# Feature-major weight chunks taken in pairs: the order of high and low products on TensorE

## The chip, the cores and the metric

One core of a Trainium2 chip runs the whole program in one launch. The metric is the device time in microseconds (us) of that launch; a lower number is better. Engines are named as in the profile: PE is TensorE (PEld its weight loads), ACT is ScalarE, DVE is VectorE, POOL is GpSimd, SP is the engine that issues the weight transfers.

## The reference, cut to what matters

Two transformer-like blocks are applied to one sequence of 256 tokens and 2048 features, all in float32. The first block normalises the input, projects it (`h @ w_in[l]`, 12040 columns), runs three sequence mixers (S5, HGRN2 and mLSTM), merges them through gates and `w_out`, and ends with a convolutional feed-forward network. The second block does the same with a dense and a dilated attention. Nearly all of the arithmetic is large matrix products with these weights:

```python
        h = rms_norm(x, mix_norm[l])
        (u_a, q_b, f_b, i_b, og_b, cx_c, v_c, o_c, ig_c, fg_c, gates) = jnp.split(h @ w_in[l], splits, axis=-1)
        ...
        x = x + merged @ w_out[l]
        x = x + conv_ffn(rms_norm(x, ffn_norm[l]), ffn_w_up[l], ffn_conv_w[l], ffn_conv_b[l], ffn_w_down[l])
```

## The kernel before, in words

**Linears, groups, chunks.** Every weight matrix is a linear with a name of its own (`w_qf`, `w_up`, `w_dn`, ...). `_linears` (L67) cuts its output columns into groups. A group of kind T ("feature-major") has two blocks of 128 output features; the weights are the stationary operand and the activations the moving one. A group of kind K ("token-major") has up to 512 output columns; there the weights move. `_chunks` (L124) cuts the input features of a group into chunks: a chunk of a T group with two blocks holds 4 input tiles of 128, so 8 pairs of (input tile, output block). A linear with 2048 input features has 4 chunks a group, one with 5632 has 11.

**High and low parts.** The float32 weights are split for accuracy. `prep` (L357) does it for one chunk: SP loads `wraw`, ACT writes the rounded part `whi` (L365), DVE writes the rest `wlo = wraw - whi` (L366). The activations are split as well: a moving operand is [high 256 | low 256] of the tokens. `mm` (L371) then issues, for a T chunk, 8 high products (`whi` against 512 moving columns, L389) and 8 low products (`wlo` against the 256 high columns, L386). The two kinds are kept in runs: `self.part` remembers which kind was issued last, and a chunk that doesn't open its accumulators begins with that kind. So chunk 0 of a group goes high, low; chunk 1 low, high; chunk 2 high, low; chunk 3 low, high; the next group begins high again. Runs are 16 long, and 8 long at the joint of two 11-chunk groups, where chunk 10 ends low and the next group has to open with high.

**The order of the program.** `run` (L457) walks over all 1009 chunks in one list, `self.seq`. For chunk i it does, in this order: `step()`, `prep` of chunk i+3, `mm` of chunk i, and behind the last chunk of a group its `evac`. All queues are in program order. `step` (L444) advances everything else by one stage: the mixers' generators ("lanes") and the deferred epilogues ("loose"). A stage can hold PE instructions, which then stand in PE's queue between the products of chunk i-1 and those of chunk i. The pools for `wraw`, `whi`, `wlo` have 4 buffers each, the accumulators 2.

**The stages that the steps of the prediction touch**, with the chunks' numbers in `self.seq`:

- `w_qf` (chunks 9 to 32), `w_cx` and `w_og` (65 to 84), beside the S5 mixer. `s5` (L912) works on 16 slices. For each it issues L1126 on PE (input products), DVE operations L1130 to L1145, and two stages after L1145 the output products L1151 on PE. In this stretch the PE stages fall on chunks 24, 28, 32, 68, 72, 76, 80, 84, between chunks 2 and 3 of a group (counted from 0).
- `w_oo` (149 to 164), beside the mLSTM mixer, whose four heads issue L1474 and L1475 on PE at chunks 150, 152, 154, 156. They need a PSUM bank that DVE's L1477 of the head before frees, and the first needs `kz`, written by ACT at L488. Two chunks later follow L1481 to L1483.
- `w_out` and `w_o`, each at the end of a branch: `turn_split` (L517) transposes the last 512 merged features on PE (L526) in the stage of chunk 1 of the first group, after DVE's L839 or L1797 has finished them and L532 has freed the PSUM bank.
- `v_c`: `norms` (L1639) sums squares over features on PE (L563) in the stage of chunk 3 of the first group, after POOL's L1613.
- `w_up` (44 groups, `ev_up` L1566): the evacuation goes ACT L405, DVE L406, DVE L416, ACT L1574, DVE L1580, ACT L1622, POOL L1624.
- `w_down` and `w_dn`: 8 groups of 11 chunks each. `w_gu` has 44 groups of 4, `w_out` and `w_o` 8, `w_qf` 6, `v_c` and `w_oo` 4, `w_cx` 3, `w_og` 2.

Of the kernel before, what the change touches and what calls it, by code (L numbers as in the profile page):

```python
# [123 lines left out]
def _chunks(lin):  # L124

    out = []
    for kind, tiles in lin["groups"]:
        widths = [len(t) for t in tiles]
        ks = np.arange(len(lin["k"]))
        n = -(-len(ks) // (1024 // sum(widths)))  # L130
        cs = [list(c) for c in np.array_split(ks, n)]
        if lin.get("early"):
            cs[:1] = [[k] for k in cs[0]]
        out.append((kind, widths, cs))
    return out
# [166 lines left out]
class Chunk:  # L302
    def __init__(self, src, off, pitch, w, mms, group):
        self.src, self.off, self.pitch, self.w, self.mms, self.group = src, off, pitch, w, mms, group
        self.first = self.last = False
        self.pre = self.post = self.hl = None


class Group:
# [4 lines left out]
class Kernel:  # L314
# [7 lines left out]
    def add(self, name, operand, evac, before=None):  # L322
        lin = LIN[name]
        nk, off = len(lin["k"]), 0
        for g, (kind, widths, chunks) in enumerate(_chunks(lin)):
            tot = sum(widths)
            grp = Group(kind, operand, (lambda *b, g=g: evac(g, *b)), (lambda g=g: before(g)) if before else None)
            for ci, ks in enumerate(chunks):
                mms = []
                for n, k in enumerate(ks):  # L330
                    c = n * tot
                    for j, w in enumerate(widths):
                        mms.append((k, j, c, w, k == 0, k == nk - 1))
                        c += w
                if ci == len(chunks) - 1:
                    mms.sort(key=lambda m: m[1] // 2)
                ch = Chunk(self.a[name], off, len(ks) * tot, len(ks) * tot, mms, grp)
                ch.first, ch.last = ci == 0, ci == len(chunks) - 1
                self.seq.append(ch)
                off += len(ks) * tot * P  # L340

# [29 lines left out]
    def mm(self, ch):  # L371


        nc, g = self.nc, ch.group
        while 2 * len(g.acc) <= max(m[1] for m in ch.mms):
            g.acc.append(self.pm.tile([P, 2, 2, S], F32, name="acc"))
        hi, lo = ch.hl
        if g.kind == "T":
            for b in range(len(g.acc)):
                mine = [m for m in ch.mms if m[1] // 2 == b]  # L380

                order = (1, 0) if self.part and not any(m[4] for m in mine) else (0, 1)
                for n, e in enumerate(order):
                    for k, j, c, w, st, en in mine:
                        if e:
                            nc.tensor.matmul(g.acc[b][:, j % 2, 0], lo[:, c:c + w], g.operand(k)[:, 0], start=False,  # L386
                                             stop=en and n == 1, skip_group_check=True)
                        else:
                            nc.tensor.matmul(g.acc[b][:, j % 2], hi[:, c:c + w], g.operand(k), start=st,  # L389
                                             stop=en and n == 1, skip_group_check=True)  # L390
                self.part = order[1]
            return
        self.part = 0
        for k, j, c, w, st, en in ch.mms:
            x = g.operand(k)
            for th in range(2):
                out = g.acc[0][:, th].rearrange("p a b -> p (a b)")[:, :w]
                t = slice(th * P, th * P + P)
                for n, (e, y) in enumerate(((0, hi), (1, hi), (0, lo))):
                    nc.tensor.matmul(out, x[:, e, t], y[:, c:c + w], start=st and n == 0, stop=en and n == 2,  # L400
                                     skip_group_check=True)
# [55 lines left out]
    def run(self):  # L457
        nxt, due = 0, 0
        for i, ch in enumerate(self.seq):
            if ch.first and ch.group.before:  # L460
                ch.group.before()
            due += ch.w
            if due >= 1024:
                self.step()
                due -= 1024
            while nxt < len(self.seq) and nxt <= i + self.LOOKAHEAD:
                self.prep(self.seq[nxt])
                nxt += 1
            self.mm(ch)
            if ch.last:  # L470
                ch.group.evac(*ch.group.acc)
        while self.loose or any(self.lanes.values()):
            self.step()
# [1154 lines left out]
    def build_second(self):  # L1628
# [163 lines left out]
        def ev_o(br, n, acc):  # L1792
            s = self.half_of(t[f"s{br}"], n)
            v.tensor_tensor(s, self.flat2(acc), s, op=OP.mult)
            if br:
                m = self.half_of(t["s0"], n)
                (v if n == 3 else gp).tensor_tensor(m, m, s, op=OP.add)  # L1797
                mm = t.setdefault("mm", [])
                mm.append(big("mm", (4, 2, S), F32R))
                self.defer(self.turn_split(mm, 4 * n, m, 1 if n == 3 else 2))  # L1800
# [292 lines left out]
```

## Time and profile before

| what | value |
|---|---|
| time, median of 3 runs | 2929.17 us (2928.81 to 2929.7) |
| the profiled execution's own time | 2929.41 us |
| its span, first to last instruction | 2927.6 us |
| PE busy | 2892.3 us, 99% of the span |
| PEld busy | 2522.4 us, 86% |
| DVE busy | 1944.2 us, 66% |
| ACT busy | 1454.2 us, 50% |
| POOL busy | 387.9 us, 13% |
| mean granted TensorE clock | 0.996 |

A busy PE is not a PE at its peak, since matmuls overlap and their ends are modelled. What counts for this kernel is the spacing of the starts of its matmuls. A line of the timeline gives the start of a run of equal instructions, the time to the end of its last one, the engine, the line of the kernel, what it writes and reads, the shape and the count; in brackets stands how long the engine was idle before it and what ended the wait. The time that a run takes of PE is the difference between its start and the start of the next run.

### The profile page before, as it was taken

Reading aid. Unit: us, or ns where it says so; the run is one execution under the profiler, and the core shown is the slowest. Engines: PE = TensorE matmul, PEld = TensorE weight load, DVE = VectorE, ACT = ScalarE, POOL = GpSimd, SP = SyncE. Lnnn points to the kernel's source line nnn. Section 1 sums busy time; section 2 is a strip of 40 time slices with the busy share of each in tenths; the row PEclk is TensorE's granted clock in tenths of the full one; section 3 lists DMA queues with packets and bytes.
Section 4 is the critical chain, followed back from the end, with each engine's and each line's share of the span. In section 5 each row is a group of like instructions: output and inputs, shape, how many; then the busy total and the mean of one; then the engine's idle time right before and its main releaser. Section 6 shows DMA issues by size and latency. Waiting matters only on the chain.

```text
span 2927.6 us, 41008 instructions
## 1 busy us (share of the span) xinstructions
PE 2892.3 (99%) x15682; PEld 2522.4 (86%) x15682; DVE 1944.2 (66%) x2536; ACT 1454.2 (50%) x2066; POOL 387.9 (13%) x412
## 2 busy tenths in 40 slices
PE   7999999999999999999999999999999999999999
PEld 6898888888888888888888988888888888888888
DVE  8998785655777777775556665565776655555444
ACT  5654545444455555554444654554544444444332
POOL 6120240011111111110111040100220000000000
PEclk9999999999999999999999999999999999999999
DMA  6565554565655555556655665565665555555664
GB/s 213 177 185 172 162 169 137 180 190 189 208 176 194 188 188 191 190 194 199 198 190 182 200 188 161 170 195 179 194 202 186 190 184 196 183 198 187 202 197 141
DMA packets 155606, 543.39 MB, mean 186 GB/s; under 512 B 17904, under 2 KB 20336, under 8 KB 155408
## 3 DMA queue, kind: packets, MB, share of 16 engines
q1 hardware_dynamic: 148752, 524.16, 55.9%
q10 hardware_dynamic: 4224, 8.21, 0.9%
q0 software_dynamic: 2432, 8.39, 0.9%
q8 instruction: 123, 2.02, 0.3%
q14 instruction: 75, 0.61, 0.1%
HBM read 534.92 MB, written 4.19 MB: 184 GB/s over the span
## 4 chain that ended last, share of the span: by engine, by line
PE 95%; DVE 3%; POOL 1%; ACT 1%; issue 1%; DMA 0%; ACTq 0%; DVEq 0%; POOLq 0%
PE acc L389 41%; PE acc L400 29%; PE acc L386 21%; PE ps_s L1298 1%; DVE wlo L366 1%; PE ps_s L1151 1%; PE ps_s L2021 0%; POOL s5p L931 0%; POOL s5p L926 0%; PE ps_s L1868 0%; PE ps_s L526 0%; ACT whi L365 0%; PE ps_s L2014 0%; PE ps_s L1949 0%; PE ps_s L1968 0%
## 5 line engine op out<-in xcount | busy, mean ns | idle before, releaser
L366 DVE TENSOR_TENSOR wlo<-wraw,whi 128x1024 fp32r<-128x1024 f32 (+3 forms) x1009 | 1261.9, 1264 | 765.8 <-ACT whi L365 760.9
L365 ACT ACTIVATE whi<-wraw 128x1024 fp32r<-128x1024 f32 (+3 forms) x1009 | 1035.0, 1040 | 854.2 <-PE acc L400 361.3
L389 PE MATMUL acc<-z,whi 128*128 128x512 f32 x2816 | 672.8, 391 | 0.0
L389 PEld LDWEIGHTS acc<-z,whi 128*128 128x128 f32 x2816 | 517.6, 188 | 100.1
L386 PEld LDWEIGHTS acc<-z,wlo 128*128 128x128 f32 x2816 | 361.0, 191 | 13.7
L386 PE MATMUL acc<-z,wlo 128*128 128x256 f32 x2816 | 365.3, 283 | 0.0
L389 PE MATMUL acc<-act,whi 128*128 128x512 f32 x1408 | 337.3, 391 | 0.0
L400 PE MATMUL acc<-whi,x 128*128 128x512 f32 (+2 forms) x1024 | 305.6, 379 | 0.0
L389 PEld LDWEIGHTS acc<-act,whi 128*128 128x128 f32 x1408 | 258.4, 188 | 49.7
L400 PE MATMUL acc<-whi,y 128*128 128x512 f32 (+2 forms) x960 | 289.3, 383 | 0.0
L1624 POOL TENSOR_TENSOR conv<-conv 128x256 f32<-128x256 f32 x88 | 100.7, 1145 | 882.1 <-ACT conv L1622 455.7
L400 PEld LDWEIGHTS acc<-whi,x 128*128 128x128 f32 x1024 | 188.8, 188 | 29.2 <-ACT whi L365 0.5
L400 PEld LDWEIGHTS acc<-whi,y 128*128 128x128 f32 x960 | 176.1, 188 | 28.3
L400 PE MATMUL acc<-wlo,x 128*128 128x512 f32 (+2 forms) x512 | 193.4, 378 | 2.1 <-DVE wlo L366 2.1
L386 PEld LDWEIGHTS acc<-act,wlo 128*128 128x128 f32 x1408 | 181.6, 191 | 7.5
L386 PE MATMUL acc<-act,wlo 128*128 128x256 f32 x1408 | 183.9, 283 | 0.0
L400 PE MATMUL acc<-wlo,y 128*128 128x512 f32 (+2 forms) x480 | 181.2, 377 | 0.0
L389 PE MATMUL acc<-x,whi 128*128 128x512 f32 x544 | 138.7, 404 | 9.7 <-ACT whi L365 6.5
L389 PEld LDWEIGHTS acc<-x,whi 128*128 128x128 f32 x544 | 103.1, 196 | 29.4 <-ACT whi L365 6.5
L400 PEld LDWEIGHTS acc<-wlo,x 128*128 128x128 f32 x512 | 96.4, 188 | 18.0 <-DVE wlo L366 2.4
L400 PEld LDWEIGHTS acc<-wlo,y 128*128 128x128 f32 x480 | 90.1, 188 | 15.6
L1622 ACT ACTIVATE conv<-conv 128x256 f32<-128x256 f32 x88 | 36.7, 418 | 131.5 <-DVE conv L1580 69.1
(455 smaller groups left out, 2901.2 us busy)
## 6 DMA issues: line engine op xcount, KB each, us to landing
wraw<-w_up SPq DMA_DIRECT2D x176, 512.0 KB, 3.7
wraw<-w_gu SPq DMA_DIRECT2D x176, 512.0 KB, 4.2
wraw<-w_down SPq DMA_DIRECT2D x88, 512.0 KB, 3.9
wraw<-w_dn SPq DMA_DIRECT2D x88, 512.0 KB, 4.0
wraw<-w_g SPq DMA_DIRECT2D x64, 512.0 KB, 3.9
wraw<-v_g SPq DMA_DIRECT2D x64, 512.0 KB, 3.5
wraw<-w_b SPq DMA_DIRECT2D x32, 512.0 KB, 4.3
wraw<-w_out SPq DMA_DIRECT2D x32, 512.0 KB, 4.0
```

The source lines that it names most:

```text
L365: nc.scalar.activation(hi[:, :w], raw[:, :w], AF.Copy)
L366: nc.vector.tensor_tensor(lo[:, :w], raw[:, :w], hi[:, :w].bitcast(F32), op=OP.subtract)
L386: nc.tensor.matmul(g.acc[b][:, j % 2, 0], lo[:, c:c + w], g.operand(k)[:, 0], start=False, stop=en and n == 1, skip_group_check=True)
L389: nc.tensor.matmul(g.acc[b][:, j % 2], hi[:, c:c + w], g.operand(k), start=st, stop=en and n == 1, skip_group_check=True)
L400: nc.tensor.matmul(out, x[:, e, t], y[:, c:c + w], start=st and n == 0, stop=en and n == 2, skip_group_check=True)
L1151: nc.tensor.matmul(py[T][:, 0], zc[:, e, 96 - 32 * j:224 - 32 * j], X[:, 3 + e], start=j + e == 0, stop=j + e == 4, skip_group_check=True)
L1298: nc.tensor.matmul(ps[:, i, b], ks[:, h, c], q[:, h, c if m < 8 else slice(P, S)], start=i + b == 0, stop=True, skip_group_check=True)
L1622: nc.scalar.activation(s, s, AF.Silu)
L1624: nc.gpsimd.tensor_tensor(s, s, c[:, 1], op=OP.mult)
```

## The change: what it does

The second chunk of each pair in a two-block T group of more than one chunk gets the first as its `mate`, and the first is `held`: its `mm` issues nothing. The `mm` of the second issues the products of both: the high ones of both chunks and then the low ones of both, or the other way round where the kind issued last was low. The eleventh chunk of an 11-chunk group stays alone. In `run` the products of a chunk with a mate are issued before the `prep` of chunk i+3 instead of behind it, because that `prep` takes the buffers of the held chunk.

```diff
 class Chunk:
-        self.pre = self.post = self.hl = None
+        self.pre = self.post = self.hl = self.mate = None
+        self.held = False
 ...
 (add)
                 ch.first, ch.last = ci == 0, ci == len(chunks) - 1
+                if kind == "T" and len(widths) == 2 and ci % 2 and not (chunks[0] is chunks[-1]):
+                    ch.mate = self.seq[-1]
+                    ch.mate.held = True
                 self.seq.append(ch)
 ...
 (mm)
-        hi, lo = ch.hl
         if g.kind == "T":
-            for b in range(len(g.acc)):
-                mine = [m for m in ch.mms if m[1] // 2 == b]
-
-                order = (1, 0) if self.part and not any(m[4] for m in mine) else (0, 1)
+            if ch.held:
+                return
+            both = [ch.mate, ch] if ch.mate else [ch]
+            tiles = [(2 * b, 2 * b + 1) for b in range(len(g.acc))]
+            for js in tiles:
+                b = js[0] // 2
+                mine = [(*x.hl, *m) for x in both for m in x.mms if m[1] in js]
+
+                order = (1, 0) if self.part and not any(m[6] for m in mine) else (0, 1)
                 for n, e in enumerate(order):
-                    for k, j, c, w, st, en in mine:
+                    for hi, lo, k, j, c, w, st, en in mine:
 ...
         self.part = 0
+        hi, lo = ch.hl
 ...
 (run)
                 self.step()
                 due -= 1024
+            if ch.mate:
+
+                self.mm(ch)
             while nxt < len(self.seq) and nxt <= i + self.LOOKAHEAD:
                 self.prep(self.seq[nxt])
                 nxt += 1
-            self.mm(ch)
+            if not ch.mate:
+                self.mm(ch)
```

## Rows read from the trace of the kernel before

**Rows 1.** The page: busy time of the engines; chain that ended last, by engine
```profile
PE 2892.3 (99%) x15682; PEld 2522.4 (86%) x15682; DVE 1944.2 (66%) x2536; ACT 1454.2 (50%) x2066; POOL 387.9 (13%) x412
...
PE 95%; DVE 3%; POOL 1%; ACT 1%; issue 1%; DMA 0%; ACTq 0%; DVEq 0%; POOLq 0%
```

**Rows 2.** Timeline of PE in `w_up` (start, us, engine, line, ...)
```profile
1199.99 3.82 PE L389 MATMUL acc<-z,whi 128*128 128x512 f32 x16
1203.65 2.08 PE L386 MATMUL acc<-z,wlo 128*128 128x256 f32 x16
1205.56 3.82 PE L389 MATMUL acc<-z,whi 128*128 128x512 f32 x16
```

**Rows 3.** Timeline of PE at the joint of two groups of `w_down`
```profile
1342.82 1.11 PE L386 MATMUL acc<-act,wlo 128*128 128x256 f32 x8
1343.77 2.00 PE L389 MATMUL acc<-act,whi 128*128 128x512 f32 x8
1345.61 1.60 PE L386 MATMUL acc<-act,wlo 128*128 128x256 f32 x12
```

**Rows 4.** Timeline of PE at the start of `w_out`
```profile
731.14 2.02 PE L389 MATMUL acc<-mo,whi 128*128 128x512 f32 x8
...
734.70 1.29 PE L526 MATMUL ps_s<-ident,m 128*128 128x128 f32 x8 [0.59 <-DVE mo L532]
```

**Rows 5.** Timeline of PE at the start of `w_o`
```profile
2095.16 1.98 PE L389 MATMUL acc<-mm,whi 128*128 128x512 f32 x8
...
2098.97 1.06 PE L526 MATMUL ps_s<-ident,m 128*128 128x128 f32 x8 [0.89 <-DVE m L1797]
```

**Rows 6.** Timeline of PE at the start of `v_c`
```profile
1558.15 2.00 PE L389 MATMUL acc<-y,whi 128*128 128x512 f32 x8
...
1566.52 1.84 PE L563 MATMUL ps_s<-ones,acc 128*128 128x1 f32 x16
```

**Rows 7.** Timeline of POOL in the same stretch
```profile
1563.93 1.94 POOL L1613 TENSOR_TENSOR acc<-acc,sq 128x512 f32<-128x512 f32 x1 [0.31 <-ACT sq L1605]
```

**Rows 8.** Timeline of PE in `w_cx` and `w_og`: S5's output products
```profile
205.40 1.02 PE L1151 MATMUL ps_s<-s5s,s5z 128*128 128x256 f32 x4
...
233.47 2.04 PE L1151 MATMUL ps_s<-s5s,s5z 128*128 128x256 f32 x4 [3.45 <-DVE s5s L1145]
...
247.38 1.02 PE L1151 MATMUL ps_s<-s5s,s5z 128*128 128x256 f32 x4
```

**Rows 9.** Timeline of DVE there: the operation that L1151 needs
```profile
203.75 0.78 DVE L1145 TENSOR_TENSOR s5s<-s5s 128x512 f32<-128x512 f32 x1
...
244.87 0.69 DVE L1145 TENSOR_TENSOR s5s<-s5s 128x512 f32<-128x512 f32 x1
```

**Rows 10.** Timeline of PE in `w_oo`
```profile
468.72 1.98 PE L389 MATMUL acc<-x,whi 128*128 128x512 f32 x8
...
472.34 0.70 PE L1475 MATMUL ps_s<-qk,kz 128*128 128x256 f32 x2 [0.27 <-ACT kz L488]
...
481.35 0.70 PE L1474 MATMUL ps_s<-qk 128*128 128x256 f32 x2 [2.31 <-DVE E L1477]
...
490.88 0.59 PE L1474 MATMUL ps_s<-qk 128*128 128x256 f32 x2
```

**Rows 11.** Timeline of DVE in `w_oo`
```profile
489.88 0.55 DVE L1477 SCALAR_TENSOR_TENSOR E<-ps_s,E 128x384 f32<-128x384 f32 x1
```

**Rows 12.** Timeline of PE in `w_qf`
```profile
65.33 1.39 PE L386 MATMUL acc<-x,wlo 128*128 128x256 f32 x8 [4.24 <-DVE wlo L366]
```

**Rows 13.** Windows: stretch, us, busy of PE, PEld, DVE, ACT, POOL, granted clock, DMA
```profile
482.60:486.00 3.40, 3.40 (x15) 3.11 (x15) 1.56 (x2) 0.00 (x0) 0.00 (x0) 0.51 0.60 169
```

**Rows 14.** Timelines of ACT and DVE in `w_up`
```profile
923.70 0.60 ACT L405 ACTIVATE pad<-acc 128x512 f32<-128x512 f32 x1 [1.99 <-PE acc L389]
...
927.86 1.23 DVE L366 TENSOR_TENSOR wlo<-wraw,whi 128x1024 fp32r<-128x1024 f32 x1 [2.11 <-ACT whi L365]
```

**Rows 15.** Groups by line and shape (count, busy us, mean ns, idle us before, releaser)
```profile
L386 PE MATMUL acc<-x,wlo 128*128 128x256 f32 x544 | 77.9, 292 | 7.5 <-DVE wlo L366 7.5
```

## The prediction

> **What bounds the kernel now.** I read the page first, for the engine that the end hangs on. PE is busy 99% of the span, and 95% of the chain that ended last lies on it [rows 1]. So the time is what PE's queue takes, instruction by instruction, and the next view is PE's timeline: the spacing in long stretches without a wait, then every place where something other than weight products stands in the queue.
>
> In `w_up`, 16 high products take 1203.65 - 1199.99 = 3.66 us of PE and 16 low ones 1205.56 - 1203.65 = 1.91 us [rows 2]: 5.57 us for two chunks, 2.78 us for one. Nothing waits there. The reader is to see that PE's other work, the mixers' small products, sits between chunks, and that it is ready with little to spare or already late when PE comes to it [rows 4 to 6, 8, 10].
>
> **The change, part by part.**
>
> *Longer runs.* The trace has no run of 32, so I extrapolate from 8 to 16. At a joint of `w_down` 8 low products take 0.95 us and 8 high ones 1.84 us [rows 3]. Twice that is 5.58 us against 5.57 us for runs of 16 [rows 2]: by kind, 3.68 against 3.66 and 1.90 against 1.91. The rounding is as large as the difference, so one pair of runs less is worth 0.01 to 0.03 us; I take 0.02. A group of 4 chunks goes from two pairs of runs to one: 6 + 3 + 2 + 4 + 8 + 44 + 4 + 8 + 44 = 123 groups, from `w_qf` to `w_gu`. A group of 11 chunks goes from six to three, and there are 16: 48 more. 171 x 0.02 = 3.4 us saved (1.7 to 5.1).
>
> By the rows the spacing in a run is 3.66 / 16 = 229 ns and 1.91 / 16 = 119 ns [rows 2], and hardly depends on the run's length. The Trainium skill (TensorE: Matmul & The Clock Gate, Back-to-back issue gap) gives 518 and 262 cycles at the full clock for 512 and 256 columns, which is 216 and 109 ns. By that the sum for two chunks would be 5.2 us, and if what is above it came from the changes of kind, halving these would return about 0.37 us for each of 171, some 63 us. The rows speak against it, since 8 or 16 in a run cost the same for each product; it is the last rival below.
>
> *What the pairing moves.* The number of products, transfers, ACT and DVE operations is unchanged, and ACT, DVE, POOL and SP keep their order; SP's transfers wait on DVE alone as before. PE's queue does change. `step()` still runs once for each chunk, but a held chunk issues nothing behind it. So PE work of a step at a held chunk stays where it was, while PE work of a step at the second of a pair now stands ahead of both chunks: a chunk earlier, 2.78 us. Such work with slack s waits max(0, 2.78 - s) longer; where it already waits, all of the 2.78 us that used to run in the shadow of the wait, or before it, is added. PE takes its queue in order, and both chunks stand behind. These are the places:
>
> - `w_out`, first group. PE comes to the first chunk at 731.14 and L526 starts at 734.70, 3.56 us later, released by DVE [rows 4]. The first chunk filled 2.78 us of this. Now nothing does: +2.78.
> - `w_o`, first group, the same with 2098.97 - 2095.16 = 3.81 us [rows 5]: +2.78.
> - `v_c`, first group. L563 started at 1566.52, after three chunks [rows 6]. It needs POOL's sum, which ends at 1563.93 + 1.94 = 1565.87 [rows 7]. PE now comes to it after two chunks, at 1558.15 + 5.57 = 1563.72: +2.1.
> - `w_cx` and `w_og`. L1145 ends at 204.53 and L1151 starts at 205.40, a slack of 0.87 us [rows 8, 9]: +1.9, and one more place like it. 40 us later the slack is 247.38 - 245.56 = 1.82 [rows 8, 9]: +1.0, and one more like it. Between them L1151 already waits 3.45 us [rows 8]: +2.78. Together 8.6. DVE's chain before that wait is busy without PE, so part of the first two is taken up there: bounds 3 and 8.6, I take 6.
> - `w_oo`. L1475 starts 3.62 us after 468.72, released by ACT, and one chunk filled 2.78 us of it [rows 10]: +2.78. L1474 at 481.35 already waits 2.31 [rows 10]; the chain behind that wait moves partly with PE: 0 to +2.8. L1474 at 490.88 [rows 10] needs L1477, which ends at 490.43 [rows 11], slack 0.45: +2.3. The fourth has slack enough. Together 5.1 to 7.9, I take 6.5 with the clock (next).
> - The clock. After PE stood still for 2.31 us [rows 10] the granted clock was 0.51 for 3.4 us [rows 13], the level of 1.2 GHz: 1.7 us lost. Waits this long or longer are now at hand at the start of `w_out`, of `w_o` and twice in `w_oo`. In the first two I add 0.9 each, half of it (bounds 0 and 1.7); in `w_oo` up to 3.4 is in the upper bound.
> - `w_qf`. A low part waits 4.24 us for DVE, and the high products of the chunk before had been done by then [rows 12]. In the pair these stand behind the late low ones: 8 x 229 ns = 1.8. Other pairs begin with high products and cover a late low part better. Bounds -1.8 and +3.7, I take +2.
>
> *Buffers.* The pair frees its 4 buffers later. The tightest place is `w_up`, where the chain after a group's end is longest. ACT L405 starts 0.21 us after the group's last product, so the end is at 923.49; the low part of the next group's chunk 3 is written at 927.86 + 1.23 = 929.09 [rows 14], 5.6 us behind it. ACT and DVE have the same order afterwards, and the weight buffer that it reuses comes free at that end in both. In a pair that begins low it is wanted 5.57 + 0.95 = 6.5 us behind the end. A slack of 0.9 us: nothing for the 44 groups, up to 1 us where DVE is behind at the stage's start. That cover is thin; a rival is made of it. `w_gu` has fewer operations in its chain.
>
> **Sum.** (2.78 + 0.9) + (2.78 + 0.9) + 2.1 + 6 + 6.5 + 2 = 24.0 us more, 3.4 less: +20.6. Against the profiled execution's own 2929.4 that is 2950.0; it lies 0.2 us above the median of the runs, so the forecast is 2949.8. The lower ends give 2.8 + 2.8 + 2.1 + 3 + 5.1 - 1.8 - 5.1 = +8.9, 2938; the upper ends 4.5 + 4.5 + 3.8 + 8.6 + 11.3 + 3.7 + 1 - 1.7 = +35.7, 2965.
>
> **The rivals.**
>
> 1. *The waits are taken up again.* While PE stands still, DVE and ACT run ahead, and later waits of PE shrink by what was lost. For it: PE already waits at several places [rows 8, 10, 12]. Against it: in `w_up`, `w_down`, `w_gu`, `w_dn` and most token-major stages PE has no waits to shrink [rows 1, 2]. It would leave at most about 6 us of the 24: 2929.2 + 6 - 3.4, some 2932, no change. Chance 0.14.
> 2. *Faster: long high runs cover late low parts.* Place: the first 120 us, where PE's low products wait 7.5 us in all for DVE [rows 15]. In pairs that begin with high products, 3.66 + 3.66 us now stand before the first low one. If all 7.5 went, and the steps' PE work were not held up: 2929.2 - 7.5 - 3.4 = 2918. It decides if the waits at the steps add less than these 11 us, for which S5's and mLSTM's steps alone are too many. Chance 0.05.
> 3. *The buffers' slack in `w_up` doesn't hold.* If the low part came 1 us after the 6.5, PE would wait 1 us in each of 44 groups: 2950 + 44 = 2994. Chance 0.03.
> 4. *The spacing in a run falls with its length.* Worked out from rows it needs two chunks to go from 5.57 us to about 5.2 in runs of 32, which from 8 to 16 they didn't begin to do [rows 2, 3]: 171 x 0.37 = 63 less, with the 24 more 2890. It is the skill's figure above taken as a mechanism. Chance 0.02.
>
> **How the numbers follow.** The forecast has 0.76. The time is its own, 2950; its own range is 2938 to 2965. To leave out no more than 2 in 10 the range goes down into the first rival: 2928 to 2963. A measurement of this kernel can tell about 0.2%, 5.9 us, from no change. Faster by more than that are rivals 2 and 4: 0.07. Within it is rival 1: 0.14. Slower are the forecast and rival 3: 0.79.
>
> **What would show it right or wrong.** In `w_up` the new timeline should show runs of 32, 7.3 and 3.8 us, and no gap between them; a gap before the low run means rival 3, a shorter run rival 4. L526 at the start of `w_out` and `w_o` should follow the token-major products with a wait of 3.5 us or more and no weight product between, with a drop of the granted clock behind it. L563 in `v_c` should wait about 2 us for POOL. L1151 in `w_cx` and `w_og` should show waits at all five places, L1474 in `w_oo` at three. From the end of `v_c` to the start of `w_o` nothing should change. If L526 still stands behind one chunk, or these waits are there and the time isn't longer, the argument is wrong.

## The result, and the profile after

The changed kernel takes 2955.16 us (median of 5 runs, 2953.31 to 2957.55), the kernel before 2929.17 us: a ratio of 1.009, 95% interval 1.0078 to 1.0101. It is slower by 26 us. The spans of the two profiled executions, 2953.4 and 2927.6 us, differ by 25.8. One execution of e6 below, of 3939 us at a granted clock of 0.68, is left out of its numbers.

Line numbers moved: L386 and L389 (low, high products) are now L394 and L397, L400 is L409, L365 and L366 are L369 and L370, L526 is L539, L563 is L576, L1145 and L1151 are L1158 and L1164, L1474, L1475 and L1477 are L1487, L1488 and L1490, L1613 is L1626.

The view that answers first is that of PE's waits: who waited, for what, total us, how often, the longest. Of the kernel before, the one line that the later text needs and the rows ahead don't have:

```profile
PE acc L400 <- DVE wlo L366: 2.1, 1, 2.1
```

Of the changed kernel:

```profile
PE ps_s L1164 <- DVE s5s L1158: 10.2, 6, 4.1
PE acc L394 <- DVE wlo L370: 10.1, 5, 6.0
...
PE ps_s L1487 <- DVE E L1490: 6.1, 3, 3.3
PE ps_s L539 <- DVE m L1810: 3.5, 1, 3.5
PE ps_s L539 <- DVE mo L545: 3.4, 1, 3.4
...
PE ps_s L1488 <- ACT kz L501: 3.0, 1, 3.0
...
PE ps_s L576 <- POOL acc L1626: 1.2, 1, 1.2
PE acc L409 <- DVE wlo L370: 0.8, 1, 0.8
```

The reader is to see that the mixers' small products now head the list: L1164 waits 10.2 us where it waited 3.45 [rows 8], the two L539 3.4 and 3.5 where L526 waited 0.59 and 0.89 [rows 4, 5], L1487 and L1488 9.1 where L1474 and L1475 waited 2.31 and 0.27 [rows 10], and L576 1.2 where L563 has no wait [rows 6]. The only wait of the kernel before that shrank by more than half a us is L409's, from 2.1 to 0.8.

PE's timeline shows the new order. In `w_up`, against [rows 2]:

```profile
929.83 7.44 PE L397 MATMUL acc<-z,whi 128*128 128x512 f32 x32
937.11 4.00 PE L394 MATMUL acc<-z,wlo 128*128 128x256 f32 x32
940.94 7.44 PE L397 MATMUL acc<-z,whi 128*128 128x512 f32 x32
```

32 high products take 937.11 - 929.83 = 7.28 us, 32 low ones 3.83, without a gap. At the start of `w_out`, against [rows 4]:

```profile
746.76 0.40 PE L409 MATMUL acc<-wlo,yc 128*128 128x512 f32 x1
750.56 1.29 PE L539 MATMUL ps_s<-ident,m 128*128 128x128 f32 x8 [3.40 <-DVE mo L545]
751.61 5.49 PE L397 MATMUL acc<-mo,whi 128*128 128x512 f32 x16
756.94 0.28 PE L394 MATMUL acc<-mo,wlo 128*128 128x256 f32 x1
```

L539 follows the token-major products directly; the 8 high and 8 low products that filled most of this wait before now stand behind it. And the 16 high products behind the wait take 756.94 - 751.61 = 5.33 us, not 3.66. The windows (columns as in [rows 13]; the granted clock is the third number from the end) say why, here and at four other places:

```profile
205.80:209.20 3.40, 3.40 (x17) 3.30 (x17) 3.27 (x3) 0.42 (x1) 3.32 (x3) 0.50 0.54 199
490.10:493.50 3.40, 3.34 (x12) 3.02 (x12) 1.65 (x2) 0.00 (x0) 0.00 (x0) 0.50 0.30 95
752.00:755.40 3.40, 3.40 (x10) 2.63 (x9) 0.21 (x1) 0.26 (x1) 0.00 (x0) 0.51 0.43 154
1588.20:1591.60 3.40, 3.40 (x17) 3.40 (x17) 2.47 (x3) 0.00 (x0) 2.78 (x4) 0.50 0.72 227
2124.10:2127.50 3.40, 3.40 (x10) 2.63 (x9) 0.00 (x0) 0.33 (x1) 2.28 (x1) 0.50 0.55 186
```

PE is busy throughout, at a granted clock of 0.50, the level of 1.2 GHz: about 1.7 us lost in each. By the trace's record of the clock, the kernel before spends 20.5 us at that level up to its last weight product, the changed kernel 37.5.

To see where the 25.8 us lie, I cut PE's timeline at the first weight product of each stage and compare lengths (a wait ahead of the first product counts for the stage before it, named in brackets):

| stage | before, us | after - before |
|---|---|---|
| `w_u`, `w_qf` | 112.59 | +2.96 |
| `w_iv` (token-major) | 77.90 | -3.05 |
| `w_cx`, `w_og` | 66.47 | +8.16 |
| start of `w_oo` (`w_g1a`) | 57.77 | +4.52 |
| `w_oo` | 58.36 | +3.53 |
| start of `w_out` (`w_b2`) | 36.18 | +4.61 |
| `w_out` | 91.25 | -0.03 |
| `w_up` | 490.78 | -0.05 |
| `w_down` | 244.99 | +0.68 |
| `v_c` | 48.16 | +2.89 |
| start of `w_o` (`w_od`) | 46.20 | +4.53 |
| `w_o` | 91.01 | -0.40 |
| `w_gu` | 490.76 | -0.87 |
| `w_dn` | 244.87 | -0.56 |
| all others together | | +0.05 |

That is 27.0; what stands ahead of the first product (-0.27) and behind the last (-1.0) closes it to the difference of the spans.

### The profile page after: what moved, and what is told of

Its sections match the earlier page's. It is cut to its first block, busy times and chain, and to the rows that moved or that the text cites. A ratio compares the mean times of both kernels' runs of the same rounds, so it can differ in the third digit from the quotient of the medians.

```text
span 2953.4 us, 41005 instructions
## 1 busy us (share of the span) xinstructions
PE 2898.4 (98%) x15682; PEld 2528.2 (86%) x15682; DVE 1934.5 (66%) x2536; ACT 1452.4 (49%) x2066; POOL 380.3 (13%) x412
## 4 chain that ended last, share of the span: by engine, by line
PE 74%; DVE 0%; ACT 0%; issue 0%; POOL 0%; ACTq 0%; POOLq 0%
PE acc L397 37%; PE acc L394 20%; PE acc L409 15%; PE ps_s L2034 0%; PE ps_s L1881 0%; DVE wlo L370 0%; PE ps_s L2027 0%; PE ps_s L1963 0%; PE ps_s L1981 0%; PE ps_s L1962 0%; PE ps_s L539 0%; PE ps_s L576 0%; ACT whi L369 0%; PE ps_s L603 0%; POOL acc L1626 0%
## 5 line engine op out<-in xcount | busy, mean ns | idle before, releaser
L370 DVE TENSOR_TENSOR wlo<-wraw,whi 128x1024 fp32r<-128x1024 f32 (+3 forms) x1009 | 1268.4, 1272 | 922.6 <-ACT whi L369 795.7
L369 ACT ACTIVATE whi<-wraw 128x1024 fp32r<-128x1024 f32 (+3 forms) x1009 | 1038.4, 1040 | 1029.2 <-PE acc L409 357.2
L397 PE MATMUL acc<-z,whi 128*128 128x512 f32 x2816 | 656.1, 390 | 0.0
L397 PEld LDWEIGHTS acc<-z,whi 128*128 128x128 f32 x2816 | 523.0, 188 | 105.0
L394 PEld LDWEIGHTS acc<-z,wlo 128*128 128x128 f32 x2816 | 349.6, 192 | 7.6 <-DVE wlo L370 0.7
L394 PE MATMUL acc<-z,wlo 128*128 128x256 f32 x2816 | 351.9, 283 | 0.5 <-DVE wlo L370 0.5
L397 PE MATMUL acc<-act,whi 128*128 128x512 f32 x1408 | 328.6, 390 | 0.0
L397 PEld LDWEIGHTS acc<-act,whi 128*128 128x128 f32 x1408 | 261.2, 188 | 52.3
L409 PE MATMUL acc<-whi,x 128*128 128x512 f32 (+2 forms) x1024 | 304.8, 379 | 0.0
L409 PE MATMUL acc<-whi,y 128*128 128x512 f32 (+2 forms) x960 | 289.3, 383 | 0.0
L409 PEld LDWEIGHTS acc<-whi,x 128*128 128x128 f32 x1024 | 188.4, 188 | 29.2 <-ACT whi L369 0.5
L409 PEld LDWEIGHTS acc<-whi,y 128*128 128x128 f32 x960 | 176.1, 188 | 28.2
L409 PE MATMUL acc<-wlo,x 128*128 128x512 f32 (+2 forms) x512 | 192.9, 377 | 0.8 <-DVE wlo L370 0.8
L409 PE MATMUL acc<-wlo,y 128*128 128x512 f32 (+2 forms) x480 | 181.2, 378 | 0.0
L394 PEld LDWEIGHTS acc<-act,wlo 128*128 128x128 f32 x1408 | 175.6, 191 | 4.6 <-DVE wlo L370 0.6
L394 PE MATMUL acc<-act,wlo 128*128 128x256 f32 x1408 | 177.6, 283 | 0.0
L397 PE MATMUL acc<-x,whi 128*128 128x512 f32 x544 | 135.0, 403 | 9.5 <-ACT whi L369 6.3
L397 PEld LDWEIGHTS acc<-x,whi 128*128 128x128 f32 x544 | 104.2, 196 | 30.2 <-ACT whi L369 6.3
L409 PEld LDWEIGHTS acc<-wlo,x 128*128 128x128 f32 x512 | 96.1, 188 | 16.5 <-DVE wlo L370 1.1
L409 PEld LDWEIGHTS acc<-wlo,y 128*128 128x128 f32 x480 | 90.1, 188 | 15.7
```

The costliest lines, as they stand in the source:

```text
L369: nc.scalar.activation(hi[:, :w], raw[:, :w], AF.Copy)
L370: nc.vector.tensor_tensor(lo[:, :w], raw[:, :w], hi[:, :w].bitcast(F32), op=OP.subtract)
```

## The experiments

Theory A: PE work of the steps stands one chunk, 2.78 us, earlier in PE's in-order queue and is not ready. Theory B: a pair frees its buffers later, so the preparation of weights is late. Theory C: waits move along the queue, so what a place loses another gains. All runs were compared with the kernel before on the same chip (its medians there: 2927.7 to 2928.0 us). The changed kernel has its 2955.16 from the measurement above, where the kernel before took 2929.17, so 1.2 to 1.5 us of a run's distance to it can come from that. Line numbers shift by a few from run to run: L1164 is L1162 in e4 and L1163 in e2, and so on.

| run | median, us | ratio to before | 95% interval |
|---|---|---|---|
| e1_step_between | 2928.96 | 1.0003 | 0.9994 to 1.0011 |
| e2_step_behind | 2922.18 | 0.998 | 0.9971 to 0.9989 |
| e3_long_stages | 2926.94 | 0.9996 | 0.9987 to 1.0004 |
| e4_old_order | 2951.1 | 1.0079 | 1.0066 to 1.0091 |
| e5_before_step_behind | 2916.88 | 0.9964 | 0.9952 to 0.9976 |
| e6_first_groups_single | 2945.34 | 1.006 | 1.0047 to 1.0073 |
| e7_behind_late_stages | 2921.97 | 0.998 | 0.9972 to 0.9989 |
| e8_runs_of_8 | 2932.8 | 1.0018 | 1.001 to 1.0027 |
| e9_behind_and_runs | 2915.8 | 0.9962 | 0.9948 to 0.9976 |

**The displacement without the long runs** (e4). From the changed kernel:

```diff
-            both = [ch.mate, ch] if ch.mate else [ch]
...
-                mine = [(*x.hl, *m) for x in both for m in x.mms if m[1] in js]
...
+            for x in ([ch.mate, ch] if ch.mate else [ch]):
+                hi, lo = x.hl
+                for b in range(len(g.acc)):
+                    mine = [m for m in x.mms if m[1] // 2 == b]
...
```

So the products of both chunks are issued at the second's place, chunk by chunk.

> Both chunks of a pair are still issued at the second chunk's place, behind its step, but one after the other, each with its own high and low runs of 16 as before. So the displacement is that of the changed kernel and the run length that of before. Theory A: the waits of the changed kernel stand, and the 3 us that longer runs save are lost: 2954 to 2960. Theory B: buffers come free chunk by chunk again, 2930 to 2940.

Measured: 2951.1 us. Theory B is out as the main cause: with the order and the run length of the kernel before, 2948.5 - 2927.6 = 20.9 of the 25.8 us remain in the spans. The waits are those of the changed kernel:

```profile
PE ps_s L1162 <- DVE s5s L1156: 10.3, 6, 4.0
...
PE ps_s L1485 <- DVE E L1488: 3.9, 2, 2.3
PE ps_s L537 <- DVE mo L543: 3.4, 1, 3.4
...
PE ps_s L1486 <- ACT kz L499: 3.0, 1, 3.0
PE ps_s L537 <- DVE m L1808: 2.9, 1, 2.9
```

A's number was too high: I expected 3 us more than the changed kernel and got 4 less (3 less if each is taken against its own kernel before). By the stages, `w_gu` and `w_dn` lost their 1.43 as expected, while `w_down` is 0.7 us shorter than after, `w_oo` 2.8 (its start is 0.8 longer), and the start of `w_o` with `w_o` itself 2.1. The latter is partly the shorter wait (2.87 against 3.55) and mostly the clock, which stayed up behind it here:

```profile
2118.20:2121.60 3.40, 3.40 (x23) 3.06 (x24) 0.92 (x1) 0.52 (x1) 0.00 (x0) 1.00 0.78 223
```

In `w_oo` L1485 waits 1.6 us at its second place where the changed kernel's waits 3.3; a stretch of half clock (0.50 from 478.8 to 481.6) lies here in front of that wait, and what is slower in front of a wait shortens it, as I read it. The record of the clock has 30.7 us at half level up to the last weight product, 6.8 less than after.

**The pairs as they are, the step's PE work elsewhere** (e1, e2). In e1 the step is issued between the first two runs of the pair:

```diff
 (mm)
                 for n, e in enumerate(order):
+                    if n and between:
+                        between()
 (run)
-            if due >= 1024:
-                self.step()
-                due -= 1024
+            now = due >= 1024
+            due -= 1024 * now
             if ch.mate:
-                self.mm(ch)
+                self.mm(ch, self.step if now else None)
+            elif now:
+                self.step()
```

In e2 the pair is issued ahead of the step:

```diff
+            if ch.mate:
+                self.mm(ch)
             if due >= 1024:
                 self.step()
                 due -= 1024
-            if ch.mate:
-                self.mm(ch)
```

> The second chunk of a pair issues its pair as before, runs of 32, but the step that falls to it is issued between the pair's two runs of the first two tiles. PE work of a step then stands behind 3.7 us (high run first) or 1.9 us (low run first) of its own pair, and no longer ahead of both chunks. Theory A (the 26 us come from PE work of steps that stands one chunk, 2.78 us, earlier in PE's queue): most of the waits that are new at L1164, L1487, L1488, L576 and L539 go or shrink by 1.9 to 3.7 us, and with the 3 us that longer runs save in the long stages the time is 2925 to 2934. Theory B (buffers come free later in a pair, and what prepares weights is late): nothing changes for the buffers, 2950 to 2957.

> The pair is issued ahead of the step that falls to its second chunk; DVE, ACT, POOL and SP keep their order. PE work of a step stands behind both chunks, one chunk later than in the kernel before. Theory A: the waits at L1164, L1487, L1488, L576 and L539 that the change brought go, and those of before shrink by up to 2.8 us each (at the start of w_out and of w_o from 3.6 and 3.8 to about 1); against it stands that mixers' results reach DVE 2.8 us later, which can bring new waits of later products for them. 2910 to 2930. Theory B: the buffers are as in the changed kernel, 2950 to 2957.

Measured: 2928.96 and 2922.18. Both keep the runs of 32 and the buffers of the changed kernel, and the order on every engine but PE. So the loss is where the step's PE work stands: half a pair later it is gone, a whole pair later there is a small gain. In e1 L1489 in `w_oo` waits 3.8 us where L1474 waited 2.31 [rows 10], and a low part waits 3.05 us at the place where L1151 waited 3.45 [rows 8], which leaves it at the time of the kernel before. In e2 no wait of L1163, L1486, L1487, L538 or L575 is left in the view; the two at L538 went altogether (my "to about 1" mistook the distance of 3.6 us for the idle 0.59 in it). What grew is another line:

```profile
PE acc L394 <- DVE wlo L370: 12.0, 8, 4.5
```

against 7.5 [rows 15]. Of this 3.0 us stand where L1151 had waited (e5, which has no pairs, waits 1.7 there), 0.9 in `v_c` and 0.5 in `w_up`. As I read it, a pair that begins low wants the second chunk's low part earlier; no run tests this alone.

**Pairs where nothing stands between chunks** (e3). From the changed kernel:

```diff
-                if kind == "T" and len(widths) == 2 and ci % 2 and not (chunks[0] is chunks[-1]):
+                if name in ("w_up", "w_down", "w_gu", "w_dn") and ci % 2:
```

> Pairs in w_up, w_down, w_gu and w_dn alone, where no mixer's product stands between chunks. Theory A: the waits of the other stages are those of the kernel before; what is left is the saving by longer runs, 0.02 us for each of 44 + 8 + 44 + some 64 pairs of runs at most, so 2926 to 2929. Theory B: these stages hold most of the pairs, and with later buffers 2945 or more.

Measured: 2926.94, as A had it, and not told apart from before by its interval. By the stages: `w_gu` -0.87, `w_dn` -0.56, `w_up` -0.03, `w_down` +0.66, the same to 0.02 as in the changed kernel. So those four numbers are the long runs and their buffers alone.

**One place at a time** (e6). The changed kernel, with the first groups of `w_out` and `w_o` unpaired:

```diff
-                if kind == "T" and len(widths) == 2 and ci % 2 and not (chunks[0] is chunks[-1]):
+                if kind == "T" and len(widths) == 2 and ci % 2 and (g or name not in ("w_out", "w_o")):
```

> The changed kernel with the pairs of the first groups of w_out and of w_o alone undone. Theory A, each place carries its own loss: L539 again stands behind one chunk, the two waits of 3.8 and 3.9 us fall to under 1 us, no half clock behind them, and 4.6 + 4.5 us come back: 2945 to 2947. If what is lost at one place is taken from or given to others (theory C, waits move along the queue), less than half of the 9 comes back, 2951 to 2955.

Measured: 2945.3, 9.8 us under the changed kernel (8.4 if each is taken against its own kernel before). PE at the start of `w_out`:

```profile
745.28 2.02 PE L397 MATMUL acc<-mo,whi 128*128 128x512 f32 x8
747.14 1.11 PE L394 MATMUL acc<-mo,wlo 128*128 128x256 f32 x8
748.85 1.29 PE L539 MATMUL ps_s<-ident,m 128*128 128x128 f32 x8 [0.59 <-DVE mo L545]
749.89 1.19 PE L394 MATMUL acc<-mo,wlo 128*128 128x256 f32 x8
750.92 3.85 PE L397 MATMUL acc<-mo,whi 128*128 128x512 f32 x16
```

The wait is the 0.59 us of [rows 4] again, and the 16 high products behind it are back at 754.62 - 750.92 = 3.70 us. The two stages' starts return 4.61 and 4.53 us to the hundredth. Theory C is out at these two places: each carries its own loss, wait and clock.

**The step's PE work later, without any pair** (e5). From the kernel before:

```diff
+            ahead = i > 0 and ch.group.kind == "T" and ch.w == 1024
+            if ahead:
+                self.mm(ch)
             if due >= 1024:
                 self.step()
 ...
-            self.mm(ch)
+            if not ahead:
+                self.mm(ch)
```

> The kernel before, without pairs, but with a full feature-major chunk's products ahead of the step that falls to it: PE work of every step stands one chunk, 2.78 us, later in PE's queue, the opposite of what the change does to half of the steps. If the place of the steps' PE work is what decides (theory A), the waits of before at L1151 (3.45 us), L1474 (2.31 us, with the half clock behind it) and L526 (0.6 and 0.9 us) go, 2918 to 2925, without any long run. If instead e2 gained by its long runs, this is no faster than before: 2926 to 2930. If mixers' results that reach DVE later make new waits, 2930 to 2945.

Measured: 2916.88, 10.8 us under the kernel before and 1.1 under the lower end that I expected, so what e2 gained was the place of the steps and not its long runs. The waits of L1151, L1474 and L526 are gone from the view, which is now short:

```profile
PE acc L386 <- DVE wlo L366: 9.0, 5, 4.3
PE acc L389 <- ACT whi L365: 6.3, 1, 6.3
PE acc L389 <- DVE u L406: 4.0, 1, 4.0
PE acc L400 <- DVE wlo L366: 2.0, 1, 2.0
PE acc L389 <- DVE qk L406: 0.7, 1, 0.7
PE ps_s L1302 <- DVE q L1291: 0.5, 1, 0.5
```

By the stages `w_oo` gives 4.29, `w_cx` and `w_og` 3.24, `w_iv` 1.89, `w_out` 0.98 and `w_o` 1.05. 4.29 is more than the waits of [rows 10]: behind 2.31 us of standing still there was also the stretch of [rows 13], and now the record of the clock has none between 70 us and the last product. The 1.89 of `w_iv` is no gain of this edit (see the last section: e3 and e8, with the code of before in that stage, have 1.59 of it), and 1.1 us of the span's 12.6 stand behind the last weight product, where runs with the same code differ by as much. What grew is L389's wait for `u`, from 3.2 to 4.0, and a low part's of 1.7 us where L1151 had waited; that mixers' results come later shows nowhere else.

**Pairs of e2 in the later stages only** (e7). From e2:

```diff
-                if kind == "T" and len(widths) == 2 and ci % 2 and not (chunks[0] is chunks[-1]):
+                if name in ("w_oo", "w_out", "w_up", "w_down", "w_o", "w_gu", "w_dn") and ci % 2:
```

> The pair ahead of its step as in e2, but pairs only in w_oo, w_out, w_up, w_down, w_o, w_gu and w_dn; w_u, w_qf, w_cx, w_og and v_c as in the kernel before. By the stages of e2's trace, w_u with w_qf gives 1.9 us back and v_c 1.4, w_cx with w_og nothing: 2918 to 2921. If the stages depend on each other (a wait returns in w_iv or at L1151), 2921 to 2926.

Measured: 2921.97, the upper case. `v_c` gave its 1.4 and the `x` stages 1.7, but L1163 waits 3.45 us again as in [rows 8], since without pairs its step is ahead of the chunk as before: +1.2 in `w_cx` and `w_og`. The span is 0.2 us under e2's, though the last weight product starts 1.2 us earlier.

**The price of a change of kind** (e8). The kernel before, with `g.plain` set for the four long stages:

```diff
-                order = (1, 0) if self.part and not any(...) else (0, 1)
+                order = (1, 0) if self.part and not g.plain and not any(...) else (0, 1)
```

> The kernel before, with high products ahead of low ones in every chunk of w_up, w_down, w_gu and w_dn, so that runs there are 8 long and not 16: 2 pairs of runs more in each of 88 groups of 4 chunks, 5 or 6 more in each of 16 groups of 11, about 264 in all. By what w_gu and w_dn of the changed kernel gave, 0.0195 us for each pair of runs: +5.1 us, 2932 to 2934. If the price of a change of kind is not the same for each (only long runs pay it back), 2928 to 2930.

Measured: 2932.8, 5.1 us over the kernel before. `w_up` and `w_gu` are longer by 1.71 each, that is 1.71 / 88 = 0.0194 us for each pair of runs, and `w_down` and `w_dn` by 0.83 each. The price is the same from 8 to 16 as from 16 to 32.

**Both together** (e9). From e5, with the `mm` of the changed kernel:

```diff
+                if (name in ("w_gu", "w_dn") or name == "w_up" and g) and ci % 2:
+                    ch.mate = self.seq[-1]
+                    ch.mate.held = True
```

> The kernel of e5 (every full feature-major chunk's products ahead of the step that falls to it) with pairs in w_gu, w_dn and all groups of w_up but the first. Long runs alone, where no buffer is late: 0.0195 us for each of 44 + 43 groups of 4 chunks and for 3 pairs of runs less in each of 8 groups of 11, so 0.0195 x (87 + 24) = 2.2 us under e5, about 2914.7. If pairs in w_up bring their wait of 0.8 us in the second group as they did in the first, 2915.5. The two gains add if the theory (place of the steps, price of a change of kind) is whole; if not, 2917 or more.

Measured: 2915.8, near the second case. Against e5, `w_gu` gives 0.83 and `w_dn` 0.56. In `w_up` there is still one wait, 41 us into the stage, as far in as in the changed kernel (884.26 there), so it was never one of the first group and leaving that unpaired did not help; it takes what 43 pairs of runs save:

```profile
849.61 3.03 PE L394 MATMUL acc<-z,wlo 128*128 128x256 f32 x24
853.15 1.22 PE L394 MATMUL acc<-z,wlo 128*128 128x256 f32 x8 [0.51 <-DVE wlo L370]
```

The two gains add in the trace (spans 2915.0 and 2913.5), but the medians lie within each other's runs. This version and e5 beat both kernels.

## Why the prediction was right, and where it was off

The forecast was 2949.8 us with its mechanism named, and the kernel takes 2955.2. By its steps, in us:

| step | predicted | stage measured | of it idle ahead of the named product | rest |
|---|---|---|---|---|
| `w_out`, L526 | 2.78 + 0.9 | 4.58 | 3.40 - 0.59 = 2.81 | 1.8 |
| `w_o`, L526 | 2.78 + 0.9 | 4.13 | 3.55 - 0.89 = 2.66 | 1.5 |
| `v_c`, L563 | 2.1 | 2.89 | 1.25 | 1.6 |
| `w_cx`, `w_og`, L1151 | 6 | 8.16 | 1.89 + 1.35 + 4.13 + 0.96 + 0.96 - 3.45 = 5.84 | 2.3 |
| `w_oo`, L1474, L1475 | 6.5 with clock | 8.05 | 3.0 + 6.1 - 0.27 - 2.31 = 6.5 | 1.5 |
| `w_qf` (with `w_u`) | 2 | 2.96 | low part 6.02 - 4.24 = 1.78, a sixth L1151 0.96 | 0.2 |
| longer runs, buffers (`w_up`, `w_down`, `w_gu`, `w_dn`) | -2.7 of the -3.4 | -0.80 | | |
| `w_iv` | 0 | -3.05 | 0.82 - 2.07 = -1.25 | -1.8 |

**The waits were right.** In the first five rows I had 20.2 us of waiting, with all of `w_oo`'s 6.5 counted as such; the idle time is 19.1. The five waits of L1151 are there, in `w_cx` and `w_og`, and a sixth ahead of them, at the end of `w_qf`, which I had not priced:

```profile
115.10 1.10 PE L1164 MATMUL ps_s<-s5s,s5z 128*128 128x256 f32 x4 [0.96 <-DVE s5s L1158]
...
204.31 1.10 PE L1164 MATMUL ps_s<-s5s,s5z 128*128 128x256 f32 x4 [1.89 <-DVE s5s L1158]
...
219.64 1.10 PE L1164 MATMUL ps_s<-s5s,s5z 128*128 128x256 f32 x4 [1.35 <-DVE s5s L1158]
...
236.20 1.74 PE L1164 MATMUL ps_s<-s5s,s5z 128*128 128x256 f32 x4 [4.13 <-DVE s5s L1158]
...
251.16 1.10 PE L1164 MATMUL ps_s<-s5s,s5z 128*128 128x256 f32 x4 [0.96 <-DVE s5s L1158]
...
264.57 1.10 PE L1164 MATMUL ps_s<-s5s,s5z 128*128 128x256 f32 x4 [0.96 <-DVE s5s L1158]
```

I had 1.9, 1.0, 1.0 and one more of 1.9 beside the one that grew by 2.78; the grown one took only 4.13 - 3.45 = 0.68, as I read it because the two ahead of it had delayed PE and let DVE catch up, the reason for which I took 6 and not 8.6. In `w_oo` and at the start of `w_o` the waits are these, the first and the third within 0.03 us of what [rows 10] and the displacement gave; the fourth head, which I had taken to have slack enough, waits 0.45:

```profile
480.15 0.70 PE L1488 MATMUL ps_s<-qk,kz 128*128 128x256 f32 x2 [3.02 <-ACT kz L501]
...
490.16 1.19 PE L1487 MATMUL ps_s<-qk 128*128 128x256 f32 x2 [3.32 <-DVE E L1490]
...
503.24 0.67 PE L1487 MATMUL ps_s<-qk 128*128 128x256 f32 x2 [2.32 <-DVE E L1490]
...
2122.88 1.06 PE L539 MATMUL ps_s<-ident,m 128*128 128x128 f32 x8 [3.55 <-DVE m L1810]
```

In `v_c` the 16 products of one line are two groups, which I had not seen:

```profile
1584.76 1.04 PE L576 MATMUL ps_s<-ones,acc 128*128 128x1 f32 x8
1587.05 1.05 PE L576 MATMUL ps_s<-ones,acc 128*128 128x1 f32 x8 [1.25 <-POOL acc L1626]
```

PE arrives 1587.05 - 1584.76 = 2.3 us ahead of POOL's release, close to the 2.1, but 8 products that don't need it fill one of these.

**The step that failed is the clock.** I put in 0.9 for each of `w_out` and `w_o`, half of what [rows 13] gives, and nothing for the other places, on the ground that the waits there were shorter than 2.31 us. The rest column is mostly what the clock took: 8.7 us in the first five rows against 1.8 in the sum. By the record of the clock each of these five places has 3.4 us more at half level than before, 1.1 us of which lie inside the wait in `w_oo`: (5 x 3.4 - 1.1) / 2 = 8.0 us lost. That is inside my bounds, whose upper ends had 1.7 for each of `w_out`, `w_o` and `v_c` and 3.4 for `w_oo`; what I took was too low. Stretches at the level of 1.2 GHz stand behind the waits in `w_out` and `w_o` in full, and also behind 1.89 us in `w_cx` and 1.25 us in `v_c`, and the one in `w_oo` is twice as long as before. e6 shows this for `w_out` and `w_o`: without the wait the stretch is gone too.

**What took part of it back** is `w_iv`, which I had left at 0: PE arrives about 3 us later, so the wait of L400 falls from 2.1 to 0.8 us. This is the first rival in one place, -1.25; elsewhere, as forecast, the long stages had no wait to shrink. The other -1.8 of that row is a stretch of half clock that the profiled execution of before had behind this wait and that e3 and e8 don't have behind the same wait (last section). So the number is nearer than its terms: the first five rows and the long stages came out some 8 us dearer than I had them, and 3 us of this came back at a place that I had put at nothing, in part by chance.

**Longer runs** are worth 0.02 us for each pair of runs (0.87 / 44 in `w_gu`), what I took, but only `w_gu` and `w_dn` got it whole. `w_up` has one wait of 0.51 us for a low part, 41 us into the stage, the "up to 1 us" of the bound, and ends at -0.05. `w_down` went up by 0.68, and there the third rival was right in kind and not in place or size: from the third group on, a low part is late in each group.

```profile
1521.07 3.05 PEld L394 LDWEIGHTS acc<-act,wlo 128*128 128x128 f32 x24
1524.28 1.01 PEld L394 LDWEIGHTS acc<-act,wlo 128*128 128x128 f32 x8 [0.16 <-DVE wlo L370]
```

By PE's timeline that run of 32 goes from 1521.29 to 1525.34, 4.05 us and not 3.83: 0.2 us a group, and not 1 us in each of 44. I had looked at `w_up` alone. That low part is late because ACT's work at a group's end stands ahead of its L369; this is read from ACT's timeline and wasn't tried.

**The other rivals.** The second, that long high runs cover late low parts, went the other way: L394's wait for `wlo` over `x` grew from 7.5 to 9.6 us (10.1 less the 0.51 in `w_up`). The wait in `w_qf` is 6.02 where it was 4.24 [rows 12], the +2 of the sum:

```profile
65.07 2.08 PE L394 MATMUL acc<-x,wlo 128*128 128x256 f32 x8 [6.02 <-DVE wlo L370]
```

The low part comes at nearly the same time (65.07 and 65.33), and e4, where the high products stand ahead of it again, waits 4.21 us there. The fourth would have needed two chunks in 5.2 us; they take 7.28 + 3.83 = 11.11 for four, 5.56 for two.

That nothing changes between the end of `v_c` and the start of `w_o` held: +0.05 us over 440.

## What to carry to other kernels

A reordering of the large products also moves the small ones that stand between them: on an engine that takes its queue in order, price every moved instruction as displacement less slack, from the rows that show its slack. Behind each wait that this makes, add the time at half clock as a cost that may come; here it was a third of the loss. And the same reading can be turned round: on a PE that is 99% busy, putting products that are ready ahead of small ones that are late gave 10.8 us, 0.4% (e5), where halving the changes of kind can give 3.4 at most.

## What the runs showed of the hardware that was not expected

- A change of kind has a price of its own, and a small one: 16 more products of a kind in a run take 7.28 - 3.66 = 3.62 us if high, 226 ns each, and 3.83 - 1.91 = 1.92 us if low, 120 ns each; a pair of runs costs about 0.02 us beyond that, at each of the lengths 8, 16 and 32 (e8, `w_gu`). The Trainium skill (TensorE: Matmul & The Clock Gate, Back-to-back issue gap) has 518 and 262 cycles for a single product of 512 and of 256 columns, 216 and 109 ns at the full clock; no run here gets there, at a granted clock of 1.00.
- The length of a wait doesn't tell whether the clock falls behind it. In the changed kernel it fell behind 1.25, 1.89, 3.40 and 3.55 us, and not behind 1.35 (at 218 us), 2.32 (at 501) or 3.02 (at 477). e4 has the waits of 2.32 and 3.02 too, and there it fell at the end of both, but not behind 2.87. And the same wait of the same code differs: L400's 2.1 us in `w_iv` are followed by 0.50 in the kernel before and by 1.00 in e8, where nothing was changed in that stage (the windows behind it, first of the kernel before, then of e8):

```profile
131.10:134.50 3.40, 3.40 (x12) 3.13 (x11) 3.40 (x7) 0.00 (x0) 0.00 (x0) 0.50 0.41 129
```

```profile
130.50:134.00 3.50, 3.44 (x19) 3.29 (x20) 3.50 (x10) 0.39 (x1) 0.00 (x0) 1.00 0.35 117
```

  So the 1.7 us behind any one wait are a chance and not a certainty, and one profile against one profile leaves that much open in each such place; the sum over the places is what the runs agree on. What decides is left open.
- A stretch at half clock that falls in front of a wait costs little: in `w_oo` the wait behind it is 1.6 us in e4 and 3.3 in the changed kernel, which has no such stretch there. In `w_qf`, e6 has the code of the changed kernel and a stretch at 0.50 from 47.1 to 50.5 us that this one lacks; there the wait for the low part is 4.57 us and not 6.02, and it ends at the same time (64.92 and 65.07).
